# A decoder step in which the ties of the sample's 256 keys are broken on VectorE, under a branch that a flag guards

## The chip, the cores and the metric

The kernel runs on one core of a Trainium2 chip. The core has a matrix engine (TensorE, PE in the profile; its weight loads are the row PEld), three engines for elementwise work (VectorE, DVE; ScalarE, ACT; GpSimd, POOL), a queue for transfers (SyncE, SP) and 16 DMA engines. Each engine takes its instructions in order and waits on semaphores for the others. The metric is the device time of one execution in microseconds, and the kernel of before stands at a median of 1019.05 us over three runs.

## The reference, cut to what matters

One layer of a decoder for a prompt of 1024 tokens and a sample of 8 sequences with 4 new tokens each. One projection feeds two groups of heads: group A attends to the 256 keys that a small indexer scores highest, group B is a retention with a recurrence over chunks of 128 tokens. The change concerns the choice of the sample's 256 keys, among 8192 past keys and the new ones:

```python
def _index_select(qi, wi, ki, qpos, kpos, topk):
    s = jnp.einsum('bqhd,bsd->bqhs', qi.astype(jnp.float32), ki.astype(jnp.float32)) * (D_IDX ** -0.5)
    score = jnp.einsum('bqh,bqhs->bqs', wi.astype(jnp.float32), jax.nn.relu(s))
    valid = kpos[None, None, :] <= qpos[None, :, None]
    score = jnp.where(valid, score, -jnp.inf)
    top_val, top_idx = lax.top_k(score, topk)
    return top_idx, jnp.isfinite(top_val)

# in _dsa_sample: topk = 256, L = 8196
    idx, ok = _index_select(qi, wi, ki_all, qpos, kpos, topk)
    ...
    kg = jnp.where(is_past[..., None, None], flat_k[phys_row].astype(ka.dtype), _gather_rows(ka, nidx))
    vg = jnp.where(is_past[..., None, None], flat_v[phys_row].astype(va.dtype), _gather_rows(va, nidx))
    return _sparse_attend(qa, kg, vg, qpos, idx, ok, rel_bias)
```

Where several keys have the same score as the 256th, top_k takes those that come first: the ties. Retention, the output projection with its norms, and a gated embedding follow.

## The kernel before, in words

All data fits one core, and the program is a sequence of stages that overlap. It projects the input for the indexer, scores the prompt's and the sample's keys, then runs four passes over the pairs of retention heads (the loop over hp), then the prompt's attention in eight query blocks, and last the output projection, the norms and the gate. Matrix products that need single precision are made of three products of split operands, which is why lines 287, 288 and 289 stand side by side in every view.

A pass hp has two halves. The qk half projects q and k for eight blocks of 128 tokens into banks named pqk (24 matmuls each); after each, VectorE turns it by its rotary angle (rope, lines 1116 to 1118, tiles rp_0 to rp_8, where rp_8 belongs to the 32 sample rows), which frees the bank, and POOL adds the two parts. Three such banks go round. The vg half projects v and the gate into banks pvg, and carries the retention of each block: two transposes (L1137, L1138), two products of q and k into the banks "ret" and "second" (L1147), on each of which VectorE lays a mask (L1148, tile sm), the state's update (L1605 on TensorE, L1610 on VectorE) and the output (L1614, L1616). Each half opens with the sample rows' own matmuls (L296).

Beside the passes run two generators that choose the sample's keys, a piece at each step. bisect_sample (bss) searches for each query's 256th score: the threshold ct. It ends beside hp=1 vg. The 8192 past scores of the 32 queries lie in Xt for it, and the program ends with a branch that a rare case guards (L1033, skipped otherwise; one like it, L767, stands at the end of the prompt's search). Then it counts how many keys lie above the threshold (count, L927), which leaves "need", the number of tied keys still to be taken, counts the tied past keys (L1067, te), and spreads the threshold and need over the partitions (tq and nq, through two transposes on TensorE, L1075). For the 32 new keys it works out which are taken, ties included (L1079 to L1084), and writes that to memory (mnew_d).

sample_select (ss) goes on from there. It loads the scores once more in another order (X, from xs_d, L1301), with a query's keys in 64 columns on each of 128 partitions, and marks the keys that equal the threshold (eq, L1326) and those above it (sel, L1327). A running sum over eq (prefix, a scan in two parts, L1338), an offset for each partition by a matmul (L1343), and three comparisons and products (L1351 to L1353) pick the first "need" of the tied keys and add them to sel. A second running sum over sel gives every chosen key its slot. The slots are then turned into row numbers in eleven groups of up to three queries (L1380 to L1394: oh on VectorE, psl on TensorE, then le, lo_, row and idx on VectorE). All these groups use one bank, so that a group's matmuls wait for the group before to be read. Last come the additive masks MA (L1403 to L1416), which need sel_d and mnew_d back from memory (sr, L1410). GpSimd gathers the key and value rows by idx (L1277); the sample's attention runs beside the prompt's.

The order of the instructions on each engine is set by a scheduler, which lays the whole program out by the dependences and its own estimates of durations; pieces of the search have priority. So a change of one piece moves others on every engine.

Of the kernel before, what the change touches and what calls it, by code (L numbers as in the profile page):

```python
# [11 lines left out]
F32 = mybir.dt.float32  # L12
# [5 lines left out]
ALU = mybir.AluOpType  # L18
AX = mybir.AxisListType
# [4 lines left out]
NS = 32  # L24
# [3 lines left out]
BIG = 1.0e30  # L28
LOW = -3.0e38
TOPK = 256  # L30
# [101 lines left out]
def tile_step(ctx: ExitStack, tc: tile.TileContext, I, O):  # L132
    nc = tc.nc
# [35 lines left out]
    ident = C("ident")  # L169
# [150 lines left out]
    nq = lp.tile([128, NS], F32, name="nq")  # L320
# [577 lines left out]
    def bisect_sample():  # L898
# [165 lines left out]
        tot = count(ct, ALU.is_gt)  # L1064
        V.tensor_scalar(need, tot, -1.0, float(TOPK), op0=ALU.mult, op1=ALU.add)

        V.tensor_scalar(jk[:, :2048], Xt[:, :2048], ct, None, op0=ALU.is_equal, op1=ALU.add, accum_out=cnt)  # L1067
# [3 lines left out]
        tf = ct[q1]  # L1071
        need, te = need[q1], te[q1]
# [4 lines left out]
        xn = Xt[:NS, 2048:]  # L1077
        sel, eq, rk = (jk.bitcast(F32)[:NS, i * NS:i * NS + NS] for i in range(3))
        V.tensor_scalar(sel, xn, tf, None, op0=ALU.is_gt)  # L1079
        V.tensor_scalar(eq, xn, tf, None, op0=ALU.is_equal)  # L1080
        V.tensor_tensor_scan(rk, eq, eq, te, op0=ALU.add, op1=ALU.bypass)
        V.scalar_tensor_tensor(eq, rk, need, eq, op0=ALU.is_le, op1=ALU.mult)
# [205 lines left out]
    def sample_select():  # L1288
# [9 lines left out]
        X = p2.tile([128, NS, 64], F32, tag="X2", name="X2")  # L1298
# [18 lines left out]
        nc.gpsimd.memset(eq66[:, :, 64:], 0.0)  # L1317
# [8 lines left out]
        V.tensor_tensor(eq, X, tqb, op=ALU.is_equal)  # L1326
# [5 lines left out]
        def prefix(src):  # L1332

            flat = src.rearrange("p q r -> p (q r)")
            to = cx.rearrange("p q r -> p (q r)")
            for c, first in ((0, 0.0), (NS * 33, to[:, NS * 33 - 1:NS * 33])):
                cs = slice(c, c + NS * 33)
                V.tensor_tensor_scan(to[:, cs], flat[:, cs], flat[:, cs], first, op0=ALU.add, op1=ALU.bypass)  # L1338
# [3 lines left out]
            t = bank("pfx", "t")  # L1342
            nc.tensor.matmul(t[:, :NS], low, tot, start=True, stop=True)  # L1343
            V.tensor_tensor(tmp, end, tot, op=ALU.subtract)
            V.tensor_copy(off, t[:, :NS])
# [5 lines left out]
        V.tensor_tensor(cx[:, :, :64], sc, lim[:, :, None].to_broadcast([128, NS, 64]), op=ALU.is_le)  # L1351
        V.tensor_tensor(eq, sc, eq, op=ALU.mult)
        V.tensor_tensor(sel, sel, eq, op=ALU.add)  # L1353
# [652 lines left out]
```

## Time and profile before

| what | us |
|---|---|
| median of three runs | 1019.05 (1011.37 to 1019.05) |
| profiled execution | 1009.07 |
| its span, first to last instruction | 1007.0 |
| mean granted TensorE clock | 0.969 of full speed |
| scores, search and passes up to the prompt's attention | 0 to 604.5 |
| prompt's attention, with the sample's | 604.5 to 770 |
| output projection, norms and gate | 770 to 1007 |

The profile is of one execution. A row of a group gives line, engine, operation, output and input tiles, shapes and count, then busy time and the mean of one in ns, then the idle time of the engine ahead of it and what ended it. A row of a timeline gives start and length in us, and in brackets the idle time ahead and its releaser. TensorE's clock is what the hardware granted, 1.00 being full speed. Matmuls overlap, so that a busy TensorE need not be at its peak.

### The profile page before, as it was taken

The numbers are of one execution on the slowest core, as the hardware profiler recorded it, in microseconds if no ns is written. First come the engines' busy times: TensorE is split into PE (matmuls) and PEld (weight loads), VectorE is DVE, ScalarE is ACT, GpSimd is POOL, SyncE is SP. The second block draws the span as 40 slices with busy tenths as digits, with TensorE's granted clock in tenths as the row PEclk, the third lists the DMA queues.
The fourth block names the chain that finished last, engine by engine and source line by source line (L and its number), as shares of the span: only waits on it lengthen the run. The fifth ranks groups of instructions, "written<-read, shape, count | busy, mean of one in ns | idle before, by whom it ended". The sixth has DMA issues, their size and how long they took to land.

```text
span 1007.0 us, 18956 instructions
## 1 busy us (share of the span) xinstructions
PE 945.4 (94%) x6983; PEld 798.3 (79%) x6983; DVE 664.2 (66%) x1936; ACT 453.5 (45%) x1005; POOL 338.8 (34%) x444
## 2 busy tenths in 40 slices
PE   4999995989999999998899988999999999999998
PEld 3989993557678988988898866566567999999998
DVE  6747667879946669889679558777754323953332
ACT  5645555345324877224422537465554434432210
POOL 4205215112406326247325226454323322233300
PEclk8999998899999999999899968999999999999999
DMA  8323234567534112032013554533221312422211
GB/s 277 100 73 102 100 111 119 188 206 255 182 104 102 41 43 69 20 91 67 24 43 102 135 162 138 163 105 97 63 79 55 112 53 84 143 86 90 86 39 37
DMA packets 102127, 104.36 MB, mean 104 GB/s; under 512 B 22002, under 2 KB 92210, under 8 KB 99602
## 3 DMA queue, kind: packets, MB, share of 16 engines
q1 hardware_dynamic: 96274, 76.93, 25.8%
q0 software_dynamic: 5760, 26.22, 8.4%
q8 instruction: 55, 0.90, 0.4%
q14 instruction: 38, 0.31, 0.1%
HBM read 80.36 MB, written 22.76 MB: 102 GB/s over the span
## 4 chain that ended last, share of the span: by engine, by line
PE 63%; DVE 14%; DMA 9%; issue 8%; POOL 3%; ACT 2%; SPq 1%; DVEq 0%; POOLq 0%; ACTq 0%
PE pb L277 5%; PE pb L278 4%; PE pb L279 4%; PE ob L1772 3%; PE ptp L1764 3%; PE pg L287 3%; PE pg L289 3%; PE pg L288 3%; PE po L287 3%; PE po L288 3%; PE po L289 3%; PE pox L877 2%; DMA kx<-in_cache_kidx,kidx 2%; PE pvg L287 2%; PE pvg L288 2%
## 5 line engine op out<-in xcount | busy, mean ns | idle before, releaser
L1277 POOL DMA_INDIRECT kvs<-in_cache_kv,idx x64 | 64.2, 1004 | 59.0 <-ACT pT L1769 32.0
L287 PE MATMUL pvg<-whi_vgb,xh 128*128 128x256 f32 x256 | 77.0, 301 | 2.5 <-DVE rp L1118 2.5
L288 PE MATMUL pvg<-wlo_vgb,xh 128*128 128x256 f32 x256 | 75.8, 296 | 0.8 <-POOL wlo_vgb L197 0.8
L287 PE MATMUL pqk<-whi_qkb,xh 128*128 128x256 f32 x256 | 73.8, 288 | 1.5 <-DVE rp L1118 1.2
L289 PE MATMUL pvg<-whi_vgb,xl 128*128 128x256 f32 x256 | 74.6, 292 | 0.0
L287 PE MATMUL po<-whi_o,yTh 128*128 128x256 f32 x256 | 73.3, 286 | 0.4 <-DVE yaT L1783 0.4
L288 PE MATMUL pqk<-wlo_qkb,xh 128*128 128x256 f32 x256 | 73.3, 287 | 0.0
L289 PE MATMUL pqk<-whi_qkb,xl 128*128 128x256 f32 x256 | 73.1, 285 | 0.0
L288 PE MATMUL po<-wlo_o,yTh 128*128 128x256 f32 x256 | 72.9, 285 | 0.0
L287 PE MATMUL pg<-whi_g,yTh 128*128 128x256 f32 x256 | 72.7, 284 | 0.0
L289 PE MATMUL po<-whi_o,yTl 128*128 128x256 f32 x256 | 72.6, 284 | 0.0
L289 PE MATMUL pg<-whi_g,yTl 128*128 128x256 f32 x256 | 72.3, 282 | 0.0
L288 PE MATMUL pg<-wlo_g,yTh 128*128 128x256 f32 x256 | 72.2, 282 | 0.0
L197 POOL TENSOR_TENSOR wlo_g<-wraw_g,whi_g 128x256 fp32r<-128x256 f32 x32 | 27.1, 881 | 88.0 <-ACT whi_g L196 87.9
L1961 DVE TENSOR_TENSOR sgm<-pu,sgm 128x256 f32<-128x256 f32 x32 | 13.6, 424 | 64.5 <-PE pu L289 61.2
L1753 ACT ACTIVATE L<-L,mn 128x128 f32<-128x128 f32 (+7 forms) x64 | 49.6, 777 | 14.5 <-DVE mn L1749 14.1
L543 DVE SCALAR_TENSOR_TENSOR score<-r,wi,score 128x384 f32<-128x384 f32 (+5 forms) x42 | 42.6, 1015 | 20.2 <-ACT r L542 18.2
L287 PEld LDWEIGHTS pvg<-whi_vgb,xh 128*128 128x128 f32 x256 | 50.0, 195 | 4.6 <-issue 2.1
L288 PEld LDWEIGHTS pvg<-wlo_vgb,xh 128*128 128x128 f32 x256 | 50.0, 195 | 1.3 <-POOL wlo_vgb L197 1.0
L287 PEld LDWEIGHTS pqk<-whi_qkb,xh 128*128 128x128 f32 x256 | 48.3, 188 | 3.1 <-issue 2.4
L287 PEld LDWEIGHTS po<-whi_o,yTh 128*128 128x128 f32 x256 | 49.0, 191 | 2.2 <-issue 1.6
L289 PEld LDWEIGHTS pvg<-whi_vgb,xl 128*128 128x128 f32 x256 | 50.1, 196 | 0.3
(559 smaller groups left out, 3115.9 us busy)
## 6 DMA issues: line engine op xcount, KB each, us to landing
wraw_qkb<-in_w_in SPq DMA_DIRECT2D x16, 256.0 KB
wraw_vgb<-in_w_in SPq DMA_DIRECT2D x16, 256.0 KB
wraw_o<-in_w_out SPq DMA_DIRECT2D x8, 512.0 KB
qas<-qas_d SPq DMA_DIRECT2D x8, 512.0 KB
xr<-in_x_prompt SPq DMA_DIRECT2D x8, 512.0 KB
wraw_g<-in_w_ple_gate SPq DMA_DIRECT2D x8, 512.0 KB
out_y_prompt<-sgm SPq DMA_DIRECT2D x32, 128.0 KB
qas_d<-qst SPq DMA_DIRECT2D x8, 384.0 KB
```

The costliest lines, as they stand in the source:

```text
L197: nc.gpsimd.tensor_tensor(lo[:, k, :n], raw, hi[:, k, :n].bitcast(F32), op=ALU.subtract)
L277: nc.tensor.matmul(pt[:m, :n], wh, xh[:, k, ts], start=(k == 0), stop=False)
L278: nc.tensor.matmul(pt[:m, :n], wh, xl[:, k, ts], start=False, stop=False)
L279: nc.tensor.matmul(pt[:m, :n], wl, xh[:, k, ts], start=False, stop=(k == KC - 1))
L287: nc.tensor.matmul(pt[:, :n], ah, hi[:, k, :n], start=(k == 0), stop=False)
L288: nc.tensor.matmul(pt[:, :n], ah, lo[:, k, :n], start=False, stop=False)
L289: nc.tensor.matmul(pt[:, :n], al, hi[:, k, :n], start=False, stop=(k == kc - 1))
L543: nc.vector.scalar_tensor_tensor(sc, r[:, :n], wi[:, qb, h:h + 1], sc if h else place[:, :n], op0=ALU.mult, op1=ALU.add)
L1277: return nc.gpsimd.indirect_dma_start(out=dst, out_offset=None, in_=kvflat, in_offset=bass.IndirectOffsetOnAxis(ap=idx, axis=0))
L1753: behind[0] = nc.scalar.activation(L[:, :n], L[:, :n], AF.Exp, bias=least, scale=-1.0, accum_out=sm[:, i4:i4 + 1])
L1764: nc.tensor.transpose(tp[:, i4 * 128:i4 * 128 + 128], P[i4][:, kb * 128:kb * 128 + 128], ident)
L1772: nc.tensor.matmul(ob[64 * o:64 * o + 64, :256], vtok[:, kb, kv * 64:kv * 64 + 64], pT[:, o * 256:o * 256 + 256], start=(kb == 0), stop=(k ...
```

## The change

The search now ends with one comparison: it counts the keys at or above the threshold, and where that is 256 no tie has to be broken. The count makes a flag (te, more than 256 for any query; "anywhere" brings the 128 partitions together with one matmul), which VectorE loads into a register. sample_select takes as chosen every key at or above the threshold (one comparison, sel), and everything that breaks ties is a function of its own, break_ties, on VectorE alone, under a branch on that flag. It sums over partitions with VectorE's 32x32 transposes and copies between quarters where the kernel before used a matmul, since it may not involve another engine. The mask of the new keys (mnew) is made in the search, in the place of six small instructions, and goes out behind the branch. The running sum is now written in place over X, in one tile X2 that is wide enough for both. Then the second running sum follows as before.

```diff
@@ bisect_sample
-        tot = count(ct, ALU.is_gt)
-        V.tensor_scalar(need, tot, -1.0, float(TOPK), op0=ALU.mult, op1=ALU.add)
-
-        V.tensor_scalar(jk[:, :2048], Xt[:, :2048], ct, None, op0=ALU.is_equal, op1=ALU.add, accum_out=cnt)
-        tot = bank("stot", "t")[:, 0:1]
-        nc.tensor.matmul(tot, group, cnt, start=True, stop=True)
-        V.tensor_copy(te, tot)
...
-        for src, dst in ((tf, tq), (need, nq)):
-            t = bank("tbc", "t")
-            nc.tensor.transpose(t[:, :NS], src.to_broadcast([NS, 128]), ident[:NS, :NS])
-            V.tensor_copy(dst, t[:, :NS])
...
-        V.tensor_scalar(sel, sel, -BIG, BIG, op0=ALU.mult, op1=ALU.add)
-        nc.sync.dma_start(mnew_d, sel)
+        tot = count(ct, ALU.is_ge)
+        V.tensor_scalar(te, tot, float(TOPK), None, op0=ALU.is_gt)
+        V.tensor_copy(tlast, ct[q1])
+        t = bank("tbc", "t")
+        nc.tensor.transpose(t[:, :NS], ct[q1].to_broadcast([NS, 128]), ident[:NS, :NS])
+        flag = anywhere(te, lp, "t")
+        next(flag)
+        V.tensor_copy(tq, t[:, :NS])
+        V.tensor_scalar(mnew, newsc, tlast, -BIG, op0=ALU.is_ge, op1=ALU.mult)
+        V.tensor_scalar(mnew, mnew, BIG, None, op0=ALU.add)
         yield
+        tied.append((yield from flag))
@@ sample_select
-        X = p2.tile([128, NS, 64], F32, tag="X2", name="X2")
+        X2 = p2.tile([128, NS * 66], F32, name="X2")
+        X = X2[:, :NS * 64].rearrange("p (q r) -> p q r", r=64)
...
-        nc.gpsimd.memset(eq66[:, :, 64:], 0.0)
...
-        V.tensor_tensor(eq, X, tqb, op=ALU.is_equal)
-        V.tensor_tensor(sel, X, tqb, op=ALU.is_gt)
-        cx = p2.tile([128, NS, 66], F32, tag="X2", name="cx")
+        cx = X2.rearrange("p (q r) -> p q r", r=66)
         sc = cx[:, :, :64]
+        V.tensor_tensor(sel, X, tqb, op=ALU.is_ge)
         yield
...
-        prefix(eq66)
-        V.tensor_tensor(lim, nq, off, op=ALU.subtract)
-        V.tensor_tensor(lim, lim, tmp, op=ALU.add)
-        yield
-        V.tensor_tensor(cx[:, :, :64], sc, lim[:, :, None].to_broadcast([128, NS, 64]), op=ALU.is_le)
-        V.tensor_tensor(eq, sc, eq, op=ALU.mult)
-        V.tensor_tensor(sel, sel, eq, op=ALU.add)
+        def break_ties():
...
+            V.tensor_tensor(eq, X, tqb, op=ALU.is_equal)
+            V.tensor_tensor(sel, X, tqb, op=ALU.is_gt)
...
+            scan(eq66)
...
+            V.tensor_tensor(sc, sc, lim[:, :, None].to_broadcast([128, NS, 64]), op=ALU.is_le)
+            V.tensor_tensor(eq, sc, eq, op=ALU.mult)
+            V.tensor_tensor(sel, sel, eq, op=ALU.add)
...
+        with tc.If(tied[0] > 0):
+            break_ties()
+        nc.sync.dma_start(mnew_d, mnew)
         nc.sync.dma_start(sel_d.rearrange("p (q r) -> p q r", r=64), sel[126:128])
         yield
-        prefix(sel66)
+        scan(sel66)
+        t = bank("pfx", "t")
+        nc.tensor.matmul(t[:, :NS], low, tot, start=True, stop=True)
+        V.tensor_tensor(tmp, end, tot, op=ALU.subtract)
+        V.tensor_copy(off, t[:, :NS])
+        yield
```

The order that the scheduler makes of it is the same on every engine up to the end of the search. Three places behind it matter. In the kernel after, lines are numbered anew: L1319 is the comparison, L1327 the scan, L1375 the branch, L1107 to L1109 the rotation, L1139 the masks, L1407 to L1421 the groups of slots.

VectorE where the selection begins, ahead of the first rotation of hp=2, before:

```order
L1326 TENSOR_TENSOR eq<-X_4178,tq 128x32x64
L1327 TENSOR_TENSOR sel<-X_4178,tq 128x32x64
L1157 BN_STATS bst<-acc_4539 128x6 x2
L1610 TENSOR_TENSOR sbd_2901<-ret,sbd_2900 64x64 x2
L1308 COPY wbias<-wb_4183 128x128
L1309 COPY wbias<-wb_4183 128x32
L1116 TENSOR_TENSOR rp_0_5355<-pqk,cst 128x256
L1117 TENSOR_TENSOR rp_0_5356<-pqk,cst 128x4x32
L1118 TENSOR_TENSOR rp_0_5356<-pqk,cst 128x4x32
L1148 TENSOR_TENSOR sm<-ret,cst 128x128
L1148 TENSOR_TENSOR sm<-second,cst 128x128
L1338 SCALAR_TENSOR_TENSOR cx<-eq 128x1056
```

and after, up to the branch:

```order
L1319 TENSOR_TENSOR sel<-X_4174,tq 128x32x64
L1148 BN_STATS bst<-acc_4564 128x6 x2
L1637 TENSOR_TENSOR sbd_2901<-ret,sbd_2902 64x64 x2
L1300 COPY wbias<-wb_4179 128x128
L1301 COPY wbias<-wb_4179 128x32
L672 TENSOR_LOAD flt
L1375 COMPARE_AND_BRANCH
```

and after, from the first instruction behind the branch on (the rows in between are break_ties):

```order
L1327 SCALAR_TENSOR_TENSOR X_4174<-sel 128x1056
L1389 CAST eq<-base 128x32 x2
L1149 BN_AGGR bmv<-bst 128x2 x2
L1139 TENSOR_TENSOR sm<-ret,cst 128x128
L301 TENSOR_TENSOR sh_qk_5342<-pqk,sh_qk_5342 32x256
L1139 TENSOR_TENSOR sm<-second,cst 128x128
L1327 SCALAR_TENSOR_TENSOR X_4174<-sel,X_4174 128x1056
L301 TENSOR_TENSOR sh_qk_5342<-pqk,sh_qk_5342 32x256
L1148 BN_STATS bst<-acc_4564 128x6 x2
L1107 TENSOR_TENSOR rp_0_5380<-pqk,cst 128x256
L1108 TENSOR_TENSOR rp_0_5381<-pqk,cst 128x4x32
L1109 TENSOR_TENSOR rp_0_5381<-pqk,cst 128x4x32
```

The scan that stood behind the rotation, over the tied keys, is gone; the scan over the chosen keys, which came a half pass later, now stands ahead of the rotation in both its parts.

SyncE's queue at the same place, before:

```order
L1033 UNCONDITIONAL_BRANCH
L1085 DMA mnew_d<-sjk 32x32
L1414 DMA MA<-mnew_d 128x1x32 x2
L1301 DMA X_4178<-xs_d 32x2048 x4
L1304 DMA wb_4183<-toep_d 32x1x132 x4
L1321 DMA dif<-in_const 128x128
L186 DMA wraw_vgb_5324<-in_w_in 128x4x128 x2
L186 DMA wraw_vgb_5327<-in_w_in 128x4x128 x2
L1633 DMA out_ret_state_prompt<-so_5195 128x64
```

and after:

```order
L1035 UNCONDITIONAL_BRANCH
L1293 DMA X_4174<-xs_d 32x2048 x4
L1296 DMA wb_4179<-toep_d 32x1x132 x4
L1312 DMA dif<-in_const 128x128
L186 DMA wraw_vgb_5349<-in_w_in 128x4x128 x2
L1375 UNCONDITIONAL_BRANCH
L1377 DMA mnew_d<-mnew 32x32
L1378 DMA sel_d<-sel 64x1x64
L186 DMA wraw_vgb_5352<-in_w_in 128x4x128 x2
L1437 DMA sr<-sel_d 128x1x64 x2
L1441 DMA MA<-mnew_d 128x1x32 x2
L1437 DMA sr<-sel_d 128x1x64 x2
```

X goes out first instead of behind mnew's write and read; mnew's write, its reads and those of sel stand behind the branch, with the second load of weights between them.

TensorE at the first group of slots (psl), before, where hp=3 qk opens with the sample row's matmuls:

```order
L289 MATMUL pvg<-whi_vgb_5322,xl 128x256
L296 MATMUL pqk<-wraw_qkb_5656,xs 32x256 x4
L296 MATMUL pqk<-wraw_qkb_5659,xs 32x256 x4
L1370 LDWEIGHTS dif_4234
L1370 MATMUL pdf<-eq,dif_4234 128x64
L1614 MATMUL ret<-sbd_2901,qkT 128x128
L1616 MATMUL ret<-vv_3_5832,sm 128x64 x2
L1382 LDWEIGHTS oh
L1382 MATMUL psl<-sel,oh 128x66
```

and after, where projections of hp=2 vg stand around it:

```order
L287 MATMUL pvg<-whi_vgb_5347,xh 128x256
L288 MATMUL pvg<-wlo_vgb_5348,xh 128x256
L289 MATMUL pvg<-whi_vgb_5347,xl 128x256
L1409 LDWEIGHTS oh
L1409 MATMUL psl<-sel,oh 128x66
```

The groups of slots have moved from hp=3 qk to hp=2 vg, a half pass sooner. After the last projection matmul of hp=3 vg and in the prompt's attention the engines' orders differ by a few rows alone.

More of the change, by code (lines that the diff above doesn't have):

```diff
@@ L319, in tile_step @@
     tq = lp.tile([128, NS], F32, name="tq")
-    nq = lp.tile([128, NS], F32, name="nq")
+    mnew = lp.tile([NS, NS], F32, name="mnew")
+    tlast = lp.tile([NS, 1], F32, name="tlast")
+    tied = []
     oaT = cp.tile([128, 4, NS], F32, name="oaT")
@@ L1325, in sample_select, with scan @@
         nc.gpsimd.tensor_copy(slot16, slots)
-        V.tensor_tensor(eq, X, tqb, op=ALU.is_equal)
-        V.tensor_tensor(sel, X, tqb, op=ALU.is_gt)
-        cx = p2.tile([128, NS, 66], F32, tag="X2", name="cx")
+        cx = X2.rearrange("p (q r) -> p q r", r=66)
         sc = cx[:, :, :64]
+        V.tensor_tensor(sel, X, tqb, op=ALU.is_ge)
         yield
-        def prefix(src):
+        def scan(src):
             flat = src.rearrange("p q r -> p (q r)")
-            to = cx.rearrange("p q r -> p (q r)")
-            for c, first in ((0, 0.0), (NS * 33, to[:, NS * 33 - 1:NS * 33])):
+            for c, first in ((0, 0.0), (NS * 33, X2[:, NS * 33 - 1:NS * 33])):
                 cs = slice(c, c + NS * 33)
-                V.tensor_tensor_scan(to[:, cs], flat[:, cs], flat[:, cs], first, op0=ALU.add, op1=ALU.bypass)
+                V.tensor_tensor_scan(X2[:, cs], flat[:, cs], flat[:, cs], first, op0=ALU.add, op1=ALU.bypass)
             V.tensor_copy(end, sc[:, :, 63])
@@ L1352, in sample_select @@
-        V.tensor_tensor(eq, sc, eq, op=ALU.mult)
-        V.tensor_tensor(sel, sel, eq, op=ALU.add)
+        def break_ties():
+            turn, run = lim, off
+            one = p2.tile([128, 8], F32, name="one")
+            group, before, need, te = (one[:, i:i + 1] for i in range(4))
+            q4 = one[:NS, 4:8]
+            quad = [slice(32 * i, 32 * i + 32) for i in range(4)]
+            V.tensor_tensor(eq, X, tqb, op=ALU.is_equal)
+            V.tensor_tensor(sel, X, tqb, op=ALU.is_gt)
+            V.memset(eq66[:, :, 64:], 0.0)
+            V.tensor_reduce(tmp, sel, axis=AX.X, op=ALU.add)
+            V.transpose(turn, tmp)
+            V.tensor_reduce(group, turn, axis=AX.X, op=ALU.add)
+            for i in range(4):
+                V.tensor_copy(q4[:, i:i + 1], group[quad[i]])
+            V.tensor_reduce(need[:NS], q4, axis=AX.X, op=ALU.add)
+            V.tensor_scalar(mnew, newsc, tlast, None, op0=ALU.is_gt, op1=ALU.add, accum_out=te[:NS])
+            V.tensor_tensor(need[:NS], need[:NS], te[:NS], op=ALU.add)
+            V.tensor_scalar(need[:NS], need[:NS], -1.0, float(TOPK), op0=ALU.mult, op1=ALU.add)
+            for i in range(1, 4):
+                V.tensor_copy(need[quad[i]], need[:NS])
+            scan(eq66)
+            V.transpose(turn, tot)
+            V.tensor_tensor_scan(run, turn, turn, 0.0, op0=ALU.add, op1=ALU.bypass)
+            V.memset(before, 0.0)
+            for i in range(3):
+                V.tensor_tensor(before[quad[i + 1]], before[quad[i]], run[quad[i], NS - 1:], op=ALU.add)
+            V.tensor_tensor(te[quad[3]], before[quad[3]], run[quad[3], NS - 1:], op=ALU.add)
+            V.tensor_copy(te[:NS], te[quad[3]])
+            V.tensor_tensor(run, run, turn, op=ALU.subtract)
+            V.tensor_scalar(run, run, before, need, op0=ALU.add, op1=ALU.subtract)
+            V.transpose(turn, run)
+            V.tensor_tensor(tmp, end, tot, op=ALU.subtract)
+            V.tensor_tensor(lim, tmp, turn, op=ALU.subtract)
+            V.tensor_tensor(sc, sc, lim[:, :, None].to_broadcast([128, NS, 64]), op=ALU.is_le)
+            V.tensor_tensor(eq, sc, eq, op=ALU.mult)
+            V.tensor_tensor(sel, sel, eq, op=ALU.add)
+            V.tensor_scalar(tmp[:NS], newsc, tlast, None, op0=ALU.is_equal)
+            V.tensor_tensor_scan(run[:NS], tmp[:NS], tmp[:NS], te[:NS], op0=ALU.add, op1=ALU.bypass)
+            V.scalar_tensor_tensor(tmp[:NS], run[:NS], need[:NS], tmp[:NS], op0=ALU.is_le, op1=ALU.mult)
+            V.tensor_tensor(mnew, mnew, tmp[:NS], op=ALU.add)
+            V.tensor_scalar(mnew, mnew, -BIG, BIG, op0=ALU.mult, op1=ALU.add)
```

11 lines of the change are left out of this document (removed).

## The prediction

> **What bounds the kernel now.** I read the page's head and its slices first, then busy time by stage, then what TensorE waits for in the stage that the change touches, and last VectorE's instructions in order of time there.
>
> The page's head gives the span, busy time by engine, and two of the rows in 40 slices of 25 us:
> ```profile
> span 1007.0 us, 18956 instructions
> PE 945.4 (94%) x6983; PEld 798.3 (79%) x6983; DVE 664.2 (66%) x1936; ACT 453.5 (45%) x1005; POOL 338.8 (34%) x444
> PE   4999995989999999998899988999999999999998
> PEclk8999998899999999999899968999999999999999
> ```
> TensorE (PE) is busy for 94% and bounds the kernel. VectorE (DVE) at 66% bounds nothing on average; its work counts only where TensorE's slices fall below 9 and the granted clock below full, slices 19 to 25, 475 to 625 us. The changed code runs just ahead of and in them.
>
> I cut that stage at TensorE's sample-row matmuls (L296), which open the qk and the vg half of each head-pair pass: hp=1 qk, hp=1 vg, hp=2 qk, hp=2 vg, hp=3 qk, hp=3 vg up to its last projection matmul, and the tail up to prompt attention. Columns: stretch, length, each engine's busy us (x instructions), granted clock, DMA:
> ```profile
> 357.00:391.90 34.90, 34.44 (x295) 30.81 (x295) 29.21 (x117) 24.94 (x51) 11.86 (x23) 1.00 0.12 33
> 391.90:430.50 38.60, 36.97 (x295) 33.16 (x294) 33.72 (x105) 17.16 (x54) 15.94 (x27) 1.00 0.27 66
> 430.50:463.50 33.00, 32.04 (x273) 28.96 (x272) 29.74 (x81) 7.53 (x19) 17.16 (x18) 1.00 0.25 59
> 463.50:506.90 43.40, 37.08 (x273) 33.80 (x272) 31.45 (x82) 20.58 (x53) 20.91 (x27) 0.92 0.21 52
> 506.90:543.00 36.10, 35.64 (x340) 32.53 (x339) 32.70 (x134) 9.36 (x27) 13.79 (x22) 1.00 0.16 42
> 543.00:581.70 38.70, 35.71 (x287) 32.64 (x287) 26.80 (x108) 18.33 (x55) 12.87 (x21) 0.96 0.55 146
> 581.70:604.50 22.80, 18.82 (x99) 14.76 (x96) 12.63 (x60) 8.28 (x20) 5.51 (x8) 0.59 0.60 173
> ```
> The reader should compare rows 2 and 4: hp=2 vg has fewer matmuls than hp=1 vg (273 against 295) and yet takes 4.8 us longer, at a clock of 0.92. What TensorE waits for from 430.5 to 604.5, engine and line, total, times, longest:
> ```profile
> PE second L1147 <- DVE sm L1148: 3.2, 2, 2.3
> PE pvg L287 <- DVE rp L1118: 1.9, 1, 1.9
> PE pcf L1404 <- DVE lo__5189 L1390: 1.5, 1, 1.5
> PE psl L1382 <- DVE lo__5094 L1390: 0.5, 1, 0.5
> ```
> All wait for VectorE. What VectorE did then, with start and length in us:
> ```profile
> 462.88 2.28 DVE L1352 TENSOR_TENSOR eq<-cx,eq 128x2048 bf16<-128x2048 f32 x1
> 466.46 0.28 DVE L1118 TENSOR_TENSOR rp<-pqk,cst 128x128 f32<-128x128 f32 x1
> 477.38 2.40 DVE L1338 TENSOR_TENSOR_SCAN cx<-sel,cx 128x1056 f32<-128x1056 bf16 x1
> 480.89 2.61 DVE L1416 TENSOR_TENSOR MA<-MA,wbias 128x160 f32<-128x160 f32 x1
> 483.53 0.29 DVE L1148 TENSOR_TENSOR sm<-second,cst 128x128 f32<-128x128 f32 x1
> ```
> L1352 is tie breaking. It holds back the rotation that frees TensorE's projection bank, the 1.9 us wait. The second scan and L1416 are selection running late behind it, and hold back the mask that frees "second", the 2.3 us wait. Then the clock halves:
> ```profile
> 480.00:485.00 5.00, 1.78 (x8) 1.42 (x9) 4.89 (x10) 3.16 (x6) 5.00 (x12) 0.83 0.19 50
> 485.00:490.00 5.00, 5.00 (x25) 5.00 (x25) 4.92 (x19) 0.50 (x2) 1.13 (x2) 0.50 0.22 64
> ```
> After five microseconds in which TensorE was busy for 1.78, 25 matmuls fill the next five, where the pace of hp=1 qk (34.9/295) fits 42.
>
> **The change, part by part.**
>
> Removed from VectorE, the large ones (line, shapes, count, busy us, mean ns):
> ```profile
> L1067 DVE TENSOR_SCALAR_CACHE_REDUCE sjk<-Xt,sbits 128x2048 bf16<-128x2048 f32 x1 | 2.3, 2336 | 0.0
> L1326 DVE TENSOR_TENSOR eq<-X,tq 128x2048 bf16<-128x2048 f32 x1 | 2.3, 2293 | 0.3 <-DMA dif<-in_const 0.3
> L1338 DVE TENSOR_TENSOR_SCAN cx<-eq 128x1056 f32<-128x1056 bf16 x1 | 2.3, 2348 | 0.0
> L1338 DVE TENSOR_TENSOR_SCAN cx<-eq,cx 128x1056 f32<-128x1056 bf16 x1 | 2.8, 2832 | 0.0
> L1351 DVE TENSOR_TENSOR cx<-cx,sm 128x2048 f32<-128x2048 f32 x1 | 2.3, 2269 | 0.0
> L1352 DVE TENSOR_TENSOR eq<-cx,eq 128x2048 bf16<-128x2048 f32 x1 | 2.3, 2283 | 0.0
> L1353 DVE TENSOR_TENSOR sel<-sel,eq 128x2048 bf16<-128x2048 bf16 x1 | 1.2, 1247 | 0.0
> ```
> They sum to 15.6 us; some fifteen small ones beside them (scan bookkeeping, masks of the new keys, copies), which I put at 0.15 to 0.5 us each, bring about 3.5 more. TensorE loses two tiny matmuls and a transpose and gains the flag's matmul; POOL loses one memset. These are nothing beside 273 matmuls a half pass.
>
> Added to VectorE: a copy, two 32x32 operations and the flag's comparison, some 0.7 us as estimated from the removed ones of like shape, and the guarded branch. Its price stands in the trace twice, as VectorE's waits at the two branches of this kind:
> ```profile
> DVE xv L858 <- DVEq L767: 1.6, 1, 1.6
> DVE ssm L1059 <- DVEq L1033: 0.8, 1, 0.8
> ```
> So 0.8 to 1.6 us; I take 0.8, since L1033 skips a body in the same stage. Behind the load stand the scan of sel, the sums of the sample row and the first rotation of hp=2, and TensorE needs the last of these. The flag's chain (count, group sum, flag matmul) is covered by the chunk steps and the 2.4 us comparison that stand ahead of the load; without that cover VectorE would wait for a place in TensorE's queue, some 3 us (24 projection matmuls of a tile at 0.12). The other four engines get a jump; TensorE's row for hp=1 vg, which holds L1033's jump, shows no cost.
>
> [...]
>
> For these inputs the branch is skipped: in the reference's own scores no query has a second key equal to its 256th. Taken, it would cost the 15.6 us above again, less L1067, and more small steps.
>
> Moved: this decides. In the order shown ahead, the selection's scans run ahead of hp=2's first rotation, and ten of its eleven groups of slots (L1380 to L1394) stand in hp=2 vg instead of hp=3 qk. Its DMAs move too: X no longer queues on SP behind the write and re-read of mnew; sel_d and the four sr loads go out as much as a half pass sooner, with the second vgb load of weights behind two small writes; the eight gathers on POOL stand ahead of hp=3's first rotation, which needs VectorE past the same groups anyway. I cost these at nothing: the weights are wanted a half pass later. One group of slots is three of the first row and one each of the others, and three small ones of 0.15:
> ```profile
> L1380 DVE TENSOR_SCALAR oh<-slot,sm 128x256 bf16<-128x256 bf16 x32 | 11.3, 405 | 1.0 <-PE psl L1382 1.0
> L1386 DVE TENSOR_TENSOR le<-psl,cst 128x384 bf16<-128x384 f32 x10 | 5.5, 547 | 0.1
> L1391 DVE TENSOR_REDUCE row<-le 128x6 f32<-128x384 bf16 x10 | 5.4, 537 | 0.0
> ```
> That is 2.75 us. Into VectorE's free time of hp=2 vg, which is cut here at its rotations:
> ```profile
> 477.20:516.80 39.60, 25.21 (x90) 0.91 0.16 42
> 516.80:552.00 35.20, 34.53 (x136) 1.00 0.23 60
> ```
> 25.2 us hold two groups (5.5), a scan, L1360, L1416 and small selection steps (10.5 together); 9.2 is left for retention, and ten groups make 36.7.
>
> The sum, half pass by half pass, against this execution:
> - hp=2 qk stays at 33.0. Between the first and third rotation VectorE now has about 12 us of work, 8 before, since MA and L1360 land there; TensorE, three banks ahead, may wait up to 2.6 us. But the 1.9 us wait at the end goes. Bounds +2.6 and -1.9; taken 0.
> - hp=2 vg: for TensorE, 273 matmuls at hp=1 vg's 131 ns (38.6/295) are 35.8, and 60 psl matmuls at 46 ns ((36.1-33.0)/(340-273)) add 2.8: 38.6. For VectorE, 36.7 and a lag of about 4 at the start: 40.7. The later ends it: -2.7. Bounds: -4.8 (TensorE alone), +2.8 (no stall goes).
> - hp=3 qk becomes like hp=2 qk, 33.0: -3.1. Bounds -3.1 and 0.
> - hp=3 vg: pcf and psl waits and one of second's (3.2-2.3), 2.9, and 0.04 of 38.7, 1.5, came with the selection's end. Bounds -4.4 and 0; taken -3.
> - tail: the same chunk steps remain after the last projection; 0, bounds -2 and +2.
>
> Together -8.8. Past 604.5 the queues are nearly the same and TensorE is the bound, so nothing is given back and nothing gained. The execution took 1009.07 us (span 1007.0), so 1000.3. The three runs lie above it, at 1011.37 to 1019.05, median 1019.05; a median of such runs I expect 2 to 10 us above, and say 5: 1005, where before would stand at 1014.
>
> **The rivals.**
> - More: TensorE no longer stalls in hp=2 vg, its clock stays full and the tail shortens: the lower bounds, -4.8 -3.1 -4.4 -2, make -14; 1000. For it: VectorE is idle for 14.4 us of 477.2 to 516.8. Against: 40.7 against 38.6 above.
> - Little: the crowding only moves. hp=2 vg keeps its 43.4 as the groups make TensorE wait in place of the scans, and only hp=3 qk gains: -3; 1011. For it: 516.8 to 552.0 shows VectorE full when it carries nine groups.
> - Slower: in hp=2 vg each of the ten groups' matmuls stands in TensorE's queue waiting for VectorE, and the ret chain behind them. If TensorE's busy share falls to that of 480 to 485, the clock halves again and again: 2.5 us for each five; eight such stretches in 40 us cost 20, less 6 gained later: +14; 1028. It decides above six stretches. Against: hp=3 qk ran the same groups at clock 1.00. [...]
> - The branch is taken after all: VectorE gets nearly all back and TensorE waits as now: +2 or more.
>
> **How the numbers follow.** Chances: the sum 0.42, more 0.20, little 0.24, slower 0.10, taken or otherwise unchanged 0.04. A measurement of this kernel can tell about 1%, 10 us, from no change. The sum's own spread of about 5 us puts half of it past that: faster 0.21+0.20, say 0.40; slower 0.10; within, 0.50. The range runs from 994 (more, with runs as quick as the quickest shown) to 1015 (little, with runs like the median), and leaves out slower and a part of the rest.
>
> **What would show it.** hp=2 vg near 40 us, hp=3 qk near 33, hp=3 vg near 35; the waits of "second" and pvg for VectorE below 3 us in all; psl in hp=2 vg; no granted clock of 0.50 ahead of the tail; a VectorE wait of about 0.8 at the new branch. I am wrong if hp=2 vg takes 43 or more, if the clock falls there, or if the tail or attention grows.

## The result, and the profile after

The changed kernel takes 989.46 us (median of 4 runs, 987.33 to 989.67), the kernel before 1015.21 us (4 runs, 1010.29 to 1019.05). The ratio is 0.9756, with a 95% interval from 0.9722 to 0.979: 25 us faster, where 9 to 10 were predicted, and below the low end of the range (994 to 1015). The profiled execution took 987.33 us. Two later runs of the kernel before, at 1290 and 1482 us with the granted clock at 0.65 and 0.56, are left out of every ratio.

The head of the page of the changed kernel, and its rows in 40 slices (of 24.6 us here):

```profile
span 985.5 us, 18931 instructions
...
PE 929.4 (94%) x6980; PEld 786.5 (80%) x6980; DVE 643.0 (65%) x1917; ACT 447.4 (45%) x1001; POOL 324.4 (33%) x443
...
PE   4999996799998999999999988999999999999998
...
PEclk8999999899999999999999969999999999999999
```

The span is 21.5 us shorter, VectorE's busy time 21.2 us (664.2 before). The reduced clock at 475 to 500 us (0.50 from 483.3 to 490.1 us before) is gone, that of the tail stays (0.50 from 573.0 to 590.1 us).

Busy time by stage, cut at the same places as before the change: hp=1 qk, hp=1 vg, hp=2 qk, hp=2 vg, hp=3 qk, hp=3 vg, the tail. Columns as in the table of before: stretch, length, busy us (x instructions) of TensorE, its weight loads, VectorE, ScalarE, GpSimd, then granted clock and DMA:

```profile
356.80:391.50 34.70, 34.19 (x290) 30.72 (x289) 28.90 (x115) 24.66 (x51) 11.85 (x23) 1.00 0.13 33
391.50:430.00 38.50, 36.82 (x296) 33.08 (x295) 32.71 (x99) 17.26 (x54) 16.10 (x27) 1.00 0.37 87
430.00:461.20 31.20, 31.20 (x276) 28.89 (x274) 28.47 (x100) 13.62 (x35) 12.09 (x23) 1.00 0.16 40
461.20:499.90 38.70, 37.70 (x342) 34.34 (x341) 31.66 (x136) 13.56 (x44) 16.92 (x27) 1.00 0.28 73
499.90:531.70 31.80, 31.80 (x283) 29.08 (x282) 27.78 (x106) 12.70 (x34) 16.94 (x31) 1.00 0.31 81
531.70:563.20 31.50, 31.50 (x269) 29.75 (x269) 11.77 (x48) 10.64 (x39) 3.36 (x8) 1.00 0.50 125
563.20:584.00 20.80, 15.10 (x104) 11.71 (x101) 14.38 (x65) 9.96 (x25) 5.71 (x8) 0.74 0.65 189
```

hp=1 is as before. From hp=2 qk to the last projection TensorE is busy for 132.2 of 133.2 us at the full clock. What it still waits for there, and what VectorE waits for in hp=2 vg and at the new branch (engine and line, releaser: total, times, longest):

```profile
PE ret L1138 <- ACT qkT L1133: 1.0, 2, 0.6
...
DVE oh L1407 <- PE psl L1409: 4.2, 5, 1.0
...
DVE X L1327 <- DVEq L1375: 0.5, 1, 0.5
```

In hp=2 vg it is now VectorE that waits for TensorE (psl, 4.2 us), no longer the other way. The new branch costs VectorE 0.5 us.

Stage by stage, from the starts of TensorE's sample-row matmuls (L296) in each trace, in us. The second row of each kernel is a later trace of the same code, the two on different chips (told of below):

| kernel | hp=2 qk | hp=2 vg | hp=3 qk | hp=3 vg | last projection to output projection |
|---|---|---|---|---|---|
| before | 33.0 | 43.5 | 36.0 | 38.7 | 205.0 |
| before, second trace | 33.2 | 42.9 | 35.9 | 38.4 | 201.7 |
| after | 31.1 | 38.7 | 31.8 | 31.5 | 202.4 |
| after, second trace | 31.1 | 38.5 | 31.8 | 31.5 | 199.9 |
| first pair, difference | -1.9 | -4.8 | -4.2 | -7.2 | -2.6 |
| predicted | 0 | -2.7 | -3.1 | -3 | 0 |

The output stage behind takes 220.3 us before and 219.9 after. All five terms were predicted too small, hp=3 vg by most. They sum to 20.7 us in the first pair of traces and to 19.3 in the second.

What the 20 us between 430 us and the tail's end are made of can be counted from the two tables of stages. Before, TensorE was busy for 159.3 of 174.0 us, and 147.2 of these remain when each stage's busy time is multiplied by its granted clock. After, it was busy for 147.3 of 154.0, and 143.4 remain. So 8.0 us of waiting are gone (14.7 against 6.7), 8.2 us of reduced clock (12.1 against 3.9), and 3.8 us of busy time at full clock, with as many matmuls (1272 and 1274). The product is rough, since the clock is also low while TensorE waits (after, from 579.8 to 583.2 us it is 0.50, and TensorE is busy for 1.54 of 3.40 us). Counted only over the time in which TensorE was busy at the reduced clock, the two traces lose 12.9 and 3.4 us, so the clock's share is 9.5 us and that of busy time at full clock 2.5.

### The profile page after: what moved, and what is told of

The parts are those of the page before. It is cut to its first block, busy times and chain, and to the rows that moved or that the text cites. A ratio compares the mean times of both kernels' runs of the same rounds, so it can differ in the third digit from the quotient of the medians.

```text
span 985.5 us, 18931 instructions
## 1 busy us (share of the span) xinstructions
PE 929.4 (94%) x6980; PEld 786.5 (80%) x6980; DVE 643.0 (65%) x1917; ACT 447.4 (45%) x1001; POOL 324.4 (33%) x443
## 4 chain that ended last, share of the span: by engine, by line
PE 75%; DMA 9%; DVE 7%; issue 3%; ACT 2%; POOL 2%; SPq 2%; ACTq 0%; DVEq 0%; POOLq 0%
PE pb L277 5%; PE pb L278 4%; PE pb L279 4%; PE ob L1799 4%; PE ptp L1791 4%; PE pg L287 3%; PE pg L289 3%; PE pg L288 3%; PE po L287 3%; PE po L289 3%; PE po L288 3%; PE pvg L287 2%; PE pvg L288 2%; PE pvg L289 2%; PE pqk L287 2%
## 5 line engine op out<-in xcount | busy, mean ns | idle before, releaser
L1268 POOL DMA_INDIRECT kvs<-in_cache_kv,idx x64 | 63.3, 989 | 85.4 <-ACT pT L1796 33.8
L288 PE MATMUL pvg<-wlo_vgb,xh 128*128 128x256 f32 x256 | 73.7, 288 | 0.8 <-POOL wlo_vgb L197 0.8
L287 PEld LDWEIGHTS pg<-whi_g,yTh 128*128 128x128 f32 x256 | 48.8, 190 | 1.6 <-issue 1.2
L544 ACT ACTIVATE r<-si 128x384 f32<-128x384 f32 (+5 forms) x48 | 35.8, 758 | 30.2 <-PE si L386 20.7
```

The source lines that it names most:

```text
L287: nc.tensor.matmul(pt[:, :n], ah, hi[:, k, :n], start=(k == 0), stop=False)
L288: nc.tensor.matmul(pt[:, :n], ah, lo[:, k, :n], start=False, stop=False)
L544: nc.scalar.activation(r[:, :n], s[:, :n], AF.Relu)
L1268: return nc.gpsimd.indirect_dma_start(out=dst, out_offset=None, in_=kvflat, in_offset=bass.IndirectOffsetOnAxis(ap=idx, axis=0))
```

## The experiments

Costs are given against the changed kernel in two ways: by the stages of the trace, and by the ratios to the kernel before (the ratio less 0.9763, times 1010 us), which carry some 5 us of uncertainty, and up to 9 in tail2, since 0.9763 itself has an interval from 0.972 to 0.9805 and each ratio has its own. The runs were made on four chips, and each ratio is to the kernel before on the same one: double, noflag, dose4 and taken; after_again, dose1, dose2 and late8; always, vg8_hp2 and vg8; vg6 and tail2. Times are compared directly only within such a group. In the edits a kernel is shown against the changed one.

| run | time, us | ratio to before, interval | by ratio |
|---|---|---|---|
| after_again | 984.23 | 0.9763, 0.972 to 0.9805 | |
| double | 984.60 | 0.9783, 0.976 to 0.9807 | +2 |
| noflag | 987.54 | 0.9814, 0.979 to 0.9839 | +5 |
| dose1 | 987.86 | 0.9801, 0.9753 to 0.9849 | +4 |
| dose2 | 989.54 | 0.981, 0.9767 to 0.9853 | +5 |
| dose4 | 994.09 | 0.9883, 0.985 to 0.9917 | +12 |
| taken | 1006.68 | 1.0003, 0.9983 to 1.0023 | +24 |
| always | 1002.30 | 0.994, 0.9915 to 0.9964 | +18 |
| late8 | 1003.25 | 0.9946, 0.9918 to 0.9975 | +18 |
| vg8_hp2 | 996.60 | 0.9875, 0.9834 to 0.9917 | +11 |
| vg8 | 996.34 | 0.9863, 0.9818 to 0.9908 | +10 |
| vg6 | 992.77 | 0.9826, 0.9757 to 0.9894 | +6 |
| tail2 | 994.69 | 0.983, 0.9755 to 0.9905 | +7 |

**The tie breaking put back, in the new order.**

```
-        V.tensor_scalar(te, tot, float(TOPK), None, op0=ALU.is_gt)
+        V.tensor_scalar(te, tot, float(TOPK - 1), None, op0=ALU.is_gt)
```

> The flag compares with 255 instead of 256, so the branch is taken and the tie breaking runs; every engine's order is that of the changed kernel, and the result is the same. It puts some 18 us of large and 4 us of small instructions back on VectorE, in one block ahead of hp=2's first rotation. Work theory (the time follows what VectorE has to do between the search and the end of hp=3): +17 to +24 us against the changed kernel's 989, so 1006 to 1013, near before. Order theory (the gain came from the scans ahead of the rotation and the slots a half pass sooner): VectorE's idle time in hp=2 and hp=3, some 34 us, takes it up but for the block itself, +2 to +8, so 991 to 997. Clock theory (the gain is mostly clock that no longer halves): a block of 22 us in which TensorE runs out of work brings the halving back, over +24.

It takes as long as the kernel before, with every engine's order that of the changed kernel. So the new order alone gains nothing once a tie breaking runs in it. It is the new formulation of it, one block from 430.7 to 452.7 us, and so not quite the old work at the old places (the run always, below, spreads it). The row of its hp=2 qk, columns as above:

```profile
430.20:484.60 54.40, 35.11 (x279) 32.44 (x280) 51.32 (x144) 13.85 (x36) 13.19 (x26) 0.78 0.09 23
```

And all that TensorE waits for in it (total, times, longest):

```profile
PE ret L1632 <- DVE sm L1139: 19.3, 1, 19.3
```

The whole cost stands in this one stage, 23.3 us more than 31.1; of the later ones hp=2 vg is 1.1 us shorter (37.6) and the others keep the changed kernel's lengths (31.8, 31.5). Hardly anything of it is taken up in VectorE's idle time behind. The wait names the reason: "ret" (L1632), the product that updates the retention's state in hp=1, stands in TensorE's queue behind the first tile of hp=2 qk. It writes into the bank "ret", and by the trace it waits for the mask (sm, L1139) that VectorE takes from that bank only after the block. Everything behind it in the queue waits, whatever banks are free: these 19.3 us are all of TensorE's idle time in the stage (54.40 less 35.11).

**The same place, in doses.** The flag is as in taken, and the branch's body is one, two or four copies of the comparison that writes sel (2.28 us each):

```
         with tc.If(tied[0] > 0):
-            break_ties()
+            [V.tensor_tensor(sel, X, tqb, op=ALU.is_ge) for _ in range(4)]; V.memset(eq66[:, :, 64:], 0.0); V.tensor_copy(mnew, mnew)
```

> The branch is taken, and its body is four copies of the comparison that writes sel (2.28 us each) and two tiny instructions: 9.3 us more on VectorE at the same place, same order, tie breaking left out. Work theory: +7 to +10 us against 989. Order theory: 0 to +3. Clock theory: no halving for so short a block, so 0 to +4, with a step between this and the full tie breaking.

> The branch is taken and its body is one copy of the comparison that writes sel and two tiny instructions: 2.5 us on VectorE ahead of hp=2's first rotation; tie breaking left out. Slack theory (TensorE has three banks of projections in hand and hides the first 2.8 us: with four copies, 9.3 us of work, it waited 6.5): 0 to +0.7 us against the changed kernel. One-for-one theory (VectorE paces the stage): +2 to +3.

> The same with two copies, 4.8 us; tie breaking left out. Slack theory: TensorE waits about 2 us, too short for the clock to halve: +1.5 to +2.5 against the changed kernel, less than half of what four copies cost (9.5), which held a halved clock of some 3 us as well. One-for-one theory: +4.5 to +5.5.

hp=2 qk takes 33.2 us with one copy, 35.3 with two, 41.0 with four, against 31.1: +2.1, +4.2 and +9.9 for 2.5, 4.8 and 9.3 us of work. Nearly one for one from the first microsecond on; the slack theory's times fall, and so does the expectation for four copies that so short a block would not halve the clock. With two copies, the row of hp=2 qk:

```profile
432.60:467.90 35.30, 33.37 (x279) 30.54 (x278) 33.11 (x104) 13.66 (x36) 12.09 (x23) 0.95 0.14 35
```

With four copies:

```profile
430.60:471.60 41.00, 34.48 (x275) 31.83 (x274) 38.37 (x106) 13.85 (x36) 12.83 (x25) 0.88 0.12 30
```

TensorE's one wait in the stage, with two copies:

```profile
PE ret L1632 <- DVE sm L1139: 1.9, 1, 1.9
```

And with four:

```profile
PE ret L1632 <- DVE sm L1139: 6.5, 1, 6.5
```

The waits are 1.9 and 6.5 us, 2.8 to 2.9 less than the work, as the slack theory had it. What it hid comes back as clock: at 0.95 and 0.88 the busy time of the two rows loses 1.7 us (0.05 of 33.37) and 4.1 us (0.12 of 34.48). So the straight line is, within a microsecond, the sum of a wait with slack (1.9 and 6.5) and of a clock that falls after it. The whole tie breaking fits too, if only the time at half clock behind its wait is counted (columns as above):

```profile
455.88:464.50 8.62, 8.62 (x40) 8.11 (x41) 8.20 (x27) 1.05 (x1) 2.65 (x5) 0.50 0.21 54
```

Half of 8.62 us and the wait of 19.3 make 23.6, against 23.3. With one copy the clock stayed at 1.00 and a projection waited 1.0 us for VectorE instead, which leaves half of its 2.1 us without an account.

**The branch.** A second guarded branch behind the first, skipped as well:

```
         with tc.If(tied[0] > 0):break_ties()
+        with tc.If(tied[0] > 0): V.memset(eq66[:, :, 64:], 0.0)
```

> A second guarded branch behind the first, on the same register, with a tiny body that is skipped too: one more compare-and-branch on VectorE and a jump on each other engine. If the branch costs what its wait shows (0.5 us on VectorE): within 1 us of the changed kernel. If the jumps on TensorE or a break in the instruction stream cost: +2 us or more.

Every engine's order is the same but for the branch itself. hp=2 qk takes 31.5 us, 0.4 more, and VectorE's wait at the two branches together is 0.8 us instead of 0.5; the intervals of the two ratios overlap. A skipped branch is nearly free here. The load of its register stands only once in this kernel, so its price was not doubled.

**Flag, branch and tie breaking left out.**

> Flag, branch and tie breaking are all left out, so ties are not broken; the scheduler is free to lay the rest out anew, and does so beside hp=1 and behind. If flag and branch cost little and the gain is the removed work, the time is within 3 us of the changed kernel whatever the order. If the order that the branch enforces made the gain, it comes out 5 us or more above it.

It comes out 3 to 5 us above the changed kernel, between the two expectations. The intervals of the ratios overlap; beside double, on the same chip, its slowest and fastest runs are 987.11 to 988.79 us against 984.26 to 985.51. The scheduler, free to mix what the branch kept apart, makes hp=2 qk 36.1 us (waits of 1.4 and 1.6 us for VectorE) and hp=3 qk 29.0. So order is worth some 5 us at most here, against the 24 of the work.

**The changed kernel, and the one before, again.**

> The changed kernel itself, on the chip of the runs beside it, as their measure: 0.973 to 0.979 of the kernel before, as when it was first timed; against the doubled branch (984.6) no more than 1 us away, since a skipped branch costs VectorE some 0.3 us.

> The kernel before, for a trace on the chip of the runs beside it: its stages from hp=2 qk to hp=3 vg within 1 us each of the first trace (33.0, 43.4, 36.1, 38.7), which makes the comparison of stages across chips fair.

The changed kernel's ratio came out as at first (0.9763). The kernel before ran once more here, at 1010.39 us; its stages from hp=2 qk to hp=3 vg agree within 1 us (table above). The stretch behind them is 3.3 us shorter, with 17.1 us at half clock where the first trace has 23.9. Unlike its first trace it has a halved clock in hp=1 vg as well, in code and order that the change doesn't touch:

```profile
391.90:435.70 43.80, 39.96 (x295) 35.91 (x294) 36.27 (x105) 17.40 (x54) 15.52 (x27) 0.92 0.23 57
```

That is 5.2 us more than the first trace's 38.6; no other trace is above that. Its other runs lie between 1004 and 1019 us, and stretches like this one are a way in which that comes about; why it struck there was not tried.

**The tie breaking always run, without a branch**, in whatever order the scheduler gives it:

```
-        with tc.If(tied[0] > 0):
-            break_ties()
+        break_ties()
```

> The changed kernel's tie breaking without the branch: it runs always, and the scheduler lays it out among the other work, with the second scan behind hp=2 vg's start as before the change. Work and place theories: 20 to 26 us slower than the changed kernel, as slow as the kernel before within 4 us. If the old formulation of the tie breaking (two more passes over the scores, one for the count and one for the offsets) was the cost and not its being run: no more than 10 us slower.

It is 18 us slower than the changed kernel, a little less than expected, and 4.5 us (0.994) faster than the kernel before. So of the 24 us about 18 come from not running the tie breaking, and some 6 from the rest of the change (the pass over the past keys that is gone, and the new form and order); these two were not separated further. The cost is spread here as it was before: 33.8, 38.2, 36.1 and 36.0 us for the four half passes, 11 us over the changed kernel, in an execution at the low end of its runs.

**Idle work behind the selection.**

```
-        s2.close()
+        [V.tensor_tensor(X, X, MA[:, 1, :64][:, None, :].to_broadcast([128, NS, 64]), op=ALU.max) for _ in range(8)]; s2.close()
```

> The changed kernel with eight idle products of 128x2048 (2.3 us each, 18 us in all, as much as the large instructions of the tie breaking) on VectorE behind the end of the selection, singly, in hp=3 qk and hp=3 vg, where VectorE was busy for 11.8 of 31.5 us. Place theory (work costs only where it stands ahead of what TensorE is about to need): 0 to +4 us against the changed kernel. Work theory (every microsecond on VectorE before the attention costs one): +14 to +20.

Eighteen microseconds of work cost 18, which speaks for the work theory. But the eight products ran from 516 to 549 us, mostly in hp=3 qk (36.6 us in place of 31.8; hp=3 vg took 35.0, and the stretch behind it 207.9), where VectorE had been busy for 27.78 of 31.80 us already, so that the place theory was not put to the test. And the edit moved TensorE's own instructions: from 518 us to the output projection only some 1040 of 1794 matmuls keep the changed kernel's order, so that the new order is a rival which this run does not exclude.

**Idle work in one half pass.** A sum over 2048 elements behind each block of the half, with hp == 3 for vg8 and hp == 2 for vg8_hp2:

```
-    met = [0]
+    met = [0]; idle = lambda hp, vv: hp == 3 and nc.vector.tensor_reduce(rt.tile([128, 16], F32, tag='dum', bufs=1, name='dum'), vv[:, None, :].to_broadcast([128, 16, 128]), axis=AX.X, op=ALU.add)
...
-            nc.scalar.copy(acc[:, tb, :], o)
+            nc.scalar.copy(acc[:, tb, :], o); idle(hp, vv)
```

> The changed kernel with one idle sum over 128x2048 (some 2.3 us on VectorE, read from each block's v) behind each of the eight blocks of hp=3 vg, 18 us in all, where VectorE was busy for 11.8 of 31.7 us. Place theory (VectorE's work costs TensorE only where VectorE is full): 0 to +4 us against the changed kernel's 984. Work theory (a microsecond on VectorE ahead of the attention costs a microsecond wherever it stands): +14 to +20.

> The same eight sums in hp=2 vg, where VectorE was busy for 31.7 of 38.7 us and the selection's groups stand. Place theory: 7 us of idle time in short pieces take up a part, and what is pushed out lands in hp=3 qk, full as well, and in hp=3 vg, which has room: +8 to +16 us, clearly more than with the sums in hp=3 vg. Work theory: +14 to +20, the same as there.

In hp=2 they cost 11 us for 18, as the place theory had it: the work is pushed on, and hp=3 qk takes 38.6 us, hp=3 vg 34.6. In hp=3 they cost 10 us by the ratios, and neither theory's number came; nor did the place theory's clear difference between the two runs (996.60 and 996.34 us, on one chip). hp=3 vg itself grew by 0.4 us only, but the stretch behind it by 7.1 (207.0 against 199.9). Two of the eight sums ran in the tail, at 572 and 580 us, so two more runs took them apart, with `idle(hp, vv)` for tb < 6 alone, and for tb > 5 alone:

> The changed kernel with the idle sums of 2.3 us behind the first six blocks of hp=3 vg only, 13.7 us in all; the two that fell into the tail in the run with eight are gone. Place theory: these six cost 0.4 us there, so 0 to +3 us against the changed kernel's 984. Work theory: +11 to +14. If the run with eight was slow for its changed order or for something ahead of the passes: +8 or more as there.

> Only the two sums behind the last two blocks, 4.6 us, which run beside the tail, where TensorE waits for VectorE in the changed kernel already and the clock is halved. Place theory: what they delay is paid at the halved clock, +5 to +9 us, more than their own length and more than the six in hp=3 vg together. Work theory: +4 to +5, a third of what the six cost.

Without the two in the tail the stretch behind hp=3 vg is still 207.6 us. The changed kernel's second trace, hp=3 vg and the 30 us behind its last projection:

```profile
531.75:563.25 31.50, 31.50 (x269) 29.78 (x269) 11.80 (x48) 10.69 (x39) 3.36 (x8) 1.00 0.49 125
563.25:593.25 30.00, 24.18 (x155) 18.10 (x154) 21.11 (x90) 15.43 (x46) 12.44 (x15) 0.72 0.58 173
```

The same two stretches with the six sums:

```profile
530.85:562.75 31.90, 31.90 (x259) 29.55 (x259) 23.48 (x48) 9.51 (x34) 3.33 (x8) 1.00 0.47 119
562.75:592.75 30.00, 24.47 (x136) 18.69 (x135) 19.76 (x86) 14.87 (x45) 9.83 (x12) 0.65 0.57 162
```

And with the two alone:

```profile
530.65:562.05 31.40, 31.40 (x269) 29.71 (x269) 13.98 (x49) 10.69 (x39) 3.35 (x8) 1.00 0.50 126
562.05:592.05 30.00, 24.11 (x142) 18.48 (x139) 21.10 (x84) 14.35 (x43) 10.77 (x13) 0.66 0.56 167
```

The reader should compare the counts. TensorE fills hp=3 vg in all three, but with six sums it gets 259 matmuls done there and not 269: eight of the retention's into the bank "ret" and two into the bank dst fall behind, into the tail, where no projections are left to run beside them and the clock is 0.65. In the first 30 us of the tail, 136 matmuls are done and not 155. So the edit in hp=3 vg was not free, though VectorE is idle there for 20 of 32 us. The six, 13.7 us long, cost 6 us by the ratios (8.1 by the stages), which neither theory had; the two, 4.6 us long and one of them still in hp=3 vg (559.4 us), cost 7 (9.7 in the stretch behind). In the eight traces in which TensorE has the changed kernel's order there, that stretch takes 198.6 to 202.4 us, so 207 to 210 stands out.

That work near the tail costs more than its own length, as the place theory had it, is not shown by this. The costs do not add: in the stretch behind hp=3 vg six sums cost 7.7 us, two cost 9.7, and all eight cost 7.1. By the ratios the six and the two cannot be told apart. And as in late8 the edits moved TensorE's own instructions: with the two sums some 800 of 1376 matmuls from 570 us to the output projection keep the changed kernel's order, with the six some 1490 of 1588 from 542 us on. The doses and taken, where every engine keeps its order, are free of this. What is common to the three runs is a longer halved clock in and behind the tail: 17.1 us in the changed kernel, 27.3 with six sums, 20.5 and 3.4 with two, 23.9 with eight. Whether VectorE's work or the new order brings it stays open.

## Why the prediction fell short

The mechanism was right: the tie breaking on VectorE held TensorE up between the search and the attention, the branch was skipped (taken, it costs 24 us), its wait was 0.5 us where 0.8 was taken, TensorE's waits for VectorE there fell below 3 us, and no halved clock is left ahead of the tail (1.00 in every half pass from hp=1 qk on). The sizes were wrong, each term of the sum on the same side. Of the 16 us between 1005 and 989, hp=3 vg has 4.2, the tail 2.6, hp=2 vg 2.1, hp=2 qk 1.9, hp=3 qk 1.1, and the allowance for the runs 2.9; about 1 lies ahead of these stages and behind them.

- **"hp=2 qk stays at 33.0."** It fell to 31.1. A wait of up to 2.6 us was feared behind three banks; there is none. The doses show that the banks give no room anyway (+2.1 us for the first 2.5 of work), and with two and four copies all that TensorE waits for is the retention's product ahead of them in its queue (1.9 and 6.5 us), but the change left VectorE in time for it.
- **"For VectorE, 36.7 and a lag of about 4: 40.7. The later ends it."** Here the step itself failed. TensorE's own sum, 38.6, is what the stage took (38.7). VectorE was busy for 31.66 us, not 36.7, and waited for TensorE: nine of the groups fell into the stage and not ten, and one of them takes 2.3 us and not 2.75 (at 482 us: 0.48, 0.28, 0.55, 0.16, 0.55, 0.17 and 0.15). The lag was no idle time to add either: the first psl matmul stands at 465.5 us, 4.3 into the stage, but VectorE was busy with other work for 3.87 of the first 4 us. That 38.6 came so close is partly luck: the stage holds 342 matmuls, not 333, and 1.0 us of waits.
- **"hp=3 qk becomes like hp=2 qk, 33.0", bound -3.1.** It took 31.8. The half pass that served as floor was itself held up: TensorE was idle for 1.0 us of its 33.0.
- **"hp=3 vg -3", bounds -4.4 and 0.** It fell by 7.2. The term's bound held the waits (2.9) and the clock (1.5), 3 of their 4.4 us were taken, and all of them came (3.0 of idle time, 1.7 of clock by the time that TensorE was busy in it). It left out the rest, 2.5 us: the selection's last matmuls are gone from the stage (16 of psl and 4 of pcf, with 287 matmuls before and 269 after). At the 46 ns that the prediction gave to one of psl these are 0.9 us; what the other 1.6 are was not tried. This is the largest miss.
- **"tail 0", bounds -2 and +2.** 2.6 us in the first pair of traces, 1.8 in the second. The same steps are left over, as predicted (1448 and 1446 matmuls up to the output projection), but in the first pair the clock is halved for 17.1 us and was for 23.9 (in the tail 0.74, and 0.59). In the second pair it is halved for 17.1 us in both, and traces with the same order of TensorE here spread over 3.8 us (198.6 to 202.4), so that this term is hardly outside its bounds.
- **The runs above their profiled execution.** 5 us were added; the four runs lie 0 to 2.3 us above it. Together with the sum, 16 us too high: 1005 against 989.

The range's low end, 994, was built on the "more" rival's -14, a sum of lower bounds. Three of its four were passed in the first pair of traces: that of hp=3 qk because it was read from a half pass of the same kernel that was held up itself, that of hp=3 vg because only waits and clock were in it, that of the tail because 2 us were too little for a clock that changes from trace to trace. The floor of hp=3 qk is what TensorE needs when nothing holds it up, 112 ns a matmul (31.80 over 283), not the 121 of hp=2 qk (33.0 over 273). The mean depends on what stands in the stage: hp=1 vg took 38.5 us after the change too, 130 ns a matmul, hp=3 vg 117 (31.50 over 269). The rival in which the clock halves in hp=2 vg didn't come: its clock is 1.00. Its premise was right in so far as the clock was worth as much as the waits (8.2 or 9.5, and 8.0 us of the gain).

## What to carry to other kernels

Where VectorE paces a stage through a chain that TensorE's queue holds in order, price removed work at its whole length first (21.2 us of VectorE, 21.5 of span here), and ask afterwards what might hide it. The whole length is shown for work that stands right ahead of what TensorE needs next (taken and the doses); spread or elsewhere it was less (18 us for the tie breaking without a branch, 11 for 18 us of sums in hp=2 vg). Idle time of VectorE in the stage is no proof that work would be hidden (20 of 32 us in hp=3 vg, where six sums of 13.7 us in all cost 6, with TensorE's order changed as well). Read the floor of a stage from one that is neither stalled nor throttled, or from TensorE's matmuls at their undisturbed pace, and never as a bound from a neighbour that suffers from the same cause. Count a wait of TensorE with the clock that it loses behind it: four copies of the comparison made it wait 6.5 us and cost 9.9, at a clock of 0.88 in the stage.

## What the runs showed of the hardware

A single wait of 1.9 us was enough to halve the clock for 3.4 us, after the wait was over. The kernel with two copies, in stretches of 2 us, columns as in the tables of stages:

```profile
438.00:440.00 2.00, 1.03 (x9) 0.81 (x7) 2.00 (x1) 0.99 (x3) 0.00 (x0) 1.00 0.17 27
440.00:442.00 2.00, 1.11 (x8) 1.00 (x8) 1.97 (x9) 0.00 (x0) 0.00 (x0) 1.00 0.89 249
442.00:444.00 2.00, 2.00 (x13) 1.80 (x13) 1.97 (x2) 1.04 (x1) 0.00 (x0) 0.63 0.14 24
444.00:446.00 2.00, 2.00 (x10) 1.81 (x10) 1.94 (x9) 0.00 (x0) 0.79 (x2) 0.51 0.00 0
446.00:448.00 2.00, 2.00 (x18) 1.89 (x17) 1.91 (x10) 0.21 (x1) 1.47 (x3) 1.00 0.08 16
```

TensorE is busy all the time again from 442 us on, and does 10 to 13 matmuls in 2 us, against 18 at full clock. The wait ended at 440.9 us, and TensorE was busy for 2.1 of the 4 us from 438 to 442. In the kernel before, a wait of 1.9 us (464.9 to 466.9 us) was followed by no drop; both happen.

In all sixteen traces, every stretch at half clock between 350 and 700 us lasts 3.4 us or a multiple of it: 3.4 with two copies, 6.8, 3.4 and 23.9 in the kernel before, 17.1 in the changed kernel, 10.2 with four copies, 27.3 with six sums, 20.5 and 3.4 with two. Those of one trace lie whole such steps apart: in the kernel before they begin at 483.3, 558.4 and 585.7 us, 22 and 8 steps of 3.41 us from one to the next. Counted in these steps from the drops, which come at 442.5 us with two copies and at 483.3 in the kernel before, the two waits fall differently. With two copies, the step ahead of the drop and the one at half clock:

```profile
439.10:442.50 3.40, 1.61 (x13) 1.36 (x14) 3.37 (x9) 0.00 (x0) 0.00 (x0) 1.00 0.65 166
442.50:445.90 3.40, 3.40 (x17) 3.15 (x16) 3.31 (x10) 1.04 (x1) 0.69 (x2) 0.51 0.06 10
```

In the kernel before, the wait lies across two steps, and no drop follows either:

```profile
462.80:466.20 3.40, 2.16 (x25) 1.21 (x23) 3.13 (x6) 0.37 (x1) 3.29 (x3) 1.00 0.19 35
466.20:469.60 3.40, 2.71 (x23) 2.75 (x24) 3.31 (x9) 1.05 (x1) 1.94 (x4) 1.00 0.57 157
```

So of two waits of 1.9 us one cost clock and the other did not; that its place in the steps decides it is an estimate from these two. A limit is not shown: in the run always, a step in which TensorE was busy for half the time (453.5 to 456.9 us, 1.70 of 3.40) was followed by the full clock, and at the start of the changed kernel's tail the clock fell behind a step with 2.81 of 3.40 busy (569.6 to 573.0 us).

The passes began between 295.6 and 300.6 us into the trace, with the same instructions ahead of them in the same order; what makes that difference was not tried. It is why stages, and not spans, are compared here.
